# Expert weights in nine wide tiles with four neighbouring rows a partition, laid over the buffers of the part before them

## Chip, core and metric

The kernel runs on one core of a Trainium2 chip. Its time is the device time of one execution in microseconds (us); a kernel is told by the median of its runs, and its profile is of one execution. The engines are named PE (matmul), DVE, ACT and POOL (elementwise), and SP, whose queue issues nearly all DMA transfers; these are carried out by the core's 16 DMA engines. All arithmetic is in float32.

## What is computed

One layer over 256 latent tokens and 256 context tokens of width 1024. Cut to what matters here:

```
mod  = silu(c) @ w_ada + b_ada                       # w_ada 1024 x 6144
z    = modulate(rms_norm(x)) @ w_in                  # w_in 1024 x 2048, also for the context
conv = silu(layer_norm(dwconv31(z0 * sigmoid(z1))))
lru  = (scan forward + scan backward)(z2, start state from the context) * gelu(z3)
x    = x + g1 * (concat(conv, lru) @ w_out)          # w_out 1024 x 1024
h2   = modulate(rms_norm(x))
top group of 4, top 2 of its 8 experts, gates
y2[t] = sum over the 2 experts e of t: gate * (silu(h2 @ w1[e]) * (h2 @ w3[e])) @ w2[e]
out  = rms_norm(x + g2 * y2)
```

There are 32 experts. Each of w1[e], w3[e] and w2[e] is 1024 x 1024, that is 4 MB, so that an expert has 12 MB and all of them 384 of the 445 MB that the core moves.

## The kernel before

**The prelude** is everything up to the router's choice: modulation, w_in, convolution, scans, w_out, router, and the gather of the tokens of the first four experts. Its order is written out by hand in the string `ORDER`, in which a letter is a step. The steps that matter here: `b` loads 1 MB of w_ada and multiplies it (line 504; the first modulation's loads are those of line 235), `s`, `t` and `i` are tap products of the convolution, `z` a projection for the gelu (line 310), `Q` and `R` the variance and the row scales of the layer norm (lines 588 and 161), `q` a square root on ACT, `n` a scan on DVE (lines 426 to 430), `L`, `I`, `J` load w_out and split it into a high and a low part (the split of line 298, for the low part on POOL), `O` the output projection (line 675), `B` brings the scales into the gather's layout (line 627), `G` and `U` gather (line 810). The instructions of each engine, and the transfers in SP's queue, run in that order; an instruction waits only for what it reads and for the buffer that it writes.

**The buffers.** All large tiles come from one pool `wp` of SLOTS = 19 tiles `slot` of 128 partitions by 2048 floats, 8 KB a partition or 1 MB, in turn. The prelude uses them for weights and for intermediate values; the experts go on in the same ring, so that a load of an expert waits for the last reader of the tile 19 allocations earlier.

**The experts** are passed in order. Experts 0 to 30 each make twelve loads of 1 MB (`up`, line 845: four for w1, four for w3, four for w2), all with

```
w = slot().rearrange("p (k n) -> p k n", k=2)
dma(w, w_d[e, k2 * 256:(k2 + 1) * 256, :].rearrange("(p k) n -> p k n", p=128))
```

Partition p so holds rows 2p and 2p + 1 of 256, which lie next to each other in memory: one run of 8 KB. The gather (`pair`, `gather_mm`) brings the tokens' columns into the same order. The matmuls of line 848 use four row pieces of a load. Tokens are gathered into `xg` for four experts at a time, and results are added to x by a matmul with a selection matrix (line 870). SP's queue has eight completion semaphores for its transfers, DMAHW0 to DMAHW7; a transfer waits until the one eight before it has landed, so at most eight are on their way.

At the end of expert 1 the largest count of tokens in an expert is reduced to one number, `fmi` (lines 1002 to 1008). At the start of what follows, `nc.values_load(fmi...)` (line 1010) reads it into a register on the engines, SP among them; it decides whether a rarely needed second part for crowded experts is run. Behind it in SP's queue stand the load of `fg` (line 1013) and the loads of expert 3 on.

**Expert 31** is cut finer, for a short tail: w1 and w3 in halves of the columns (`up_half`, line 1032, 16 loads of 512 KB in runs of 2 KB), w2 in four loads of 512 KB of whole rows (line 1080) and four of 512 KB in column pieces (`part`, line 1089, runs of 1 KB). Between them PE finishes a piece, and DVE, ACT and POOL the normalisation of its columns.

Of the kernel before, what the change touches and what calls it, by code (L numbers as in the profile page):

```python
# [7 lines left out]
F32 = mybir.dt.float32  # L8
# [7 lines left out]
D = 1024  # L16
# [5 lines left out]
SLOTS = 19  # L22
# [8 lines left out]
v0 v1 h0 h1 o0 l0 t*2 v3 o1 t*3 v2 u0 l3 t*2 l1 l2 u1 t*2 b t s t s t*2 b t s t*2 s t s*3 t s*2 t s t i t s t s*2 t i  # L31
t*2 c1 t*2 b t s*2 t*3 s*2 t s b s*3 t*2 c0 b s*2 u2 s c2 s p10 s i p00 b a10 t*2 i*3 a00 u3 t p11 t s t w i t*3 b p01
t p20 s c3 s t s t s p30 t*2 d10 s t s*2 i t*2 a20 s*2 a30 t b t d00 t p21 a01 t r1 b t*2 s q10 t d30 i t d20 i b s b
t*2 s L0 q30 s q20 t s t*3 q00 z0 t L4 t b z1 t i p31 t*2 n00 s t*2 n20 d01 M a11 a31 k1 I0 C2 L2 z2 n10 C1 a21 I2 C0
C3 d21 d11 b q21 q11 q01 d31 Q z3 b R n01 e0 N1 L6 N2 x X1 N0 b X2 N3 I4 X3 b n30 n11 X0 m0 J0 J2 O001 e3 O002 J4 O100
q31 O111 O102 O112 O000 O011 e1 O012 I6 O010 O003 g n21 n31 O110 e2 O113 J6 j m1 X5 O101 m3 m2 X4 X7 X6 r2 O103 O005
O007 O013 O006 O105 O004 O015 O106 k2 O016 O114 O104 O017 O014 O107 D00 O115 D01 y H00 Y0 D10 O117 O116 H01 H10 D11
K00 H11 K01 Z0 K10 K11 T0 P0 F0 G06 B G04 G02 G00 Y1 T1 G07 P1 Z1 G03 F1 G01 G05 G10 G11 G12 G16 G14 A1 U0 G17 G15 U1
U4 G13 U2 U3 U6 U5 A0 U7
# [7 lines left out]
LNSQ = "SGGG"  # L47
XC = ("SS", "SV")
WH, WL = "VSVS", "VVGV"
MH, ML = "VSSGGSSG", "GVGGGVVG"  # L50
# [12 lines left out]
NSP = _n  # L63
# [3 lines left out]
def hybrid_layer(ctx: ExitStack, tc: tile.TileContext, sp_d, x_d, c_d, bada_d, rb_d, fg_d, gw_d,  # L67
                 wada_d, win_d, wout_d, w1_d, w3_d, w2_d, out_d):
    nc = tc.nc
    V, S, G, P = nc.vector, nc.scalar, nc.gpsimd, nc.tensor  # L70
    dma = nc.sync.dma_start

    const = ctx.enter_context(tc.tile_pool(name="const", bufs=1))
    wp = ctx.enter_context(tc.tile_pool(name="wp", bufs=SLOTS))
# [5 lines left out]
    def slot():  # L80
        return wp.tile([128, 2048], F32, name="slot")

    ctx.enter_context(tc.manual_schedule())
# [3 lines left out]
    sp = const.tile([128, NSP], F32, name="sp")  # L87
# [6 lines left out]
    bada = const.tile([48, 128], F32, name="bada")  # L94
# [9 lines left out]
    xn = const.tile([128, 2, D], F32, name="xn")  # L104
# [83 lines left out]
    silc = const.tile([128, 8, 32], F32, name="silc")  # L188
# [126 lines left out]
    pt = ada_turn(ada_rows(pa))  # L315
# [289 lines left out]
    wrs = const.tile([128, 8, 36], F32, name="wrs")  # L605
# [17 lines left out]
    def paired():  # L623
        pt = bank()
        for i in range(2):
            for h in range(2):
                P.matmul(pt[64 * h:64 * h + 64, i * 8:(i + 1) * 8], ident[:, i::2], gs[:, :, h::2],
                         start=i == 0, stop=i == 1, skip_group_check=True, tile_position=(0, 64 * h))
        S.copy(gsp.rearrange("p j (a i) -> p i j a", i=2), pt[:, 0:16].rearrange("p (i j a) -> p i j a", i=2, j=2))
# [149 lines left out]
    def pair(k):  # L779

        return slice(k // 2 * 256 + k % 2, k // 2 * 256 + 256, 2)

    def gather_mm(pg, i, k, oh, t):
        P.matmul(pg[:, i * 256:(i + 1) * 256], xn[:, t, pair(k)],  # L784
                 oh[:, t].rearrange("p e s -> p (e s)"), start=t + i == 0, stop=t == 1 and i == 1,
                 skip_group_check=True)
# [30 lines left out]
    def route(t):  # L817
# [7 lines left out]
                 g=g1_rows, B=paired, I=wo_hi, J=wo_lo, X=mixt_split, Z=first_split, y=second, x=router_row, j=router_rows, L=load_wo, O=oproj, W=warm,  # L825
# [12 lines left out]

    mo = ctx.enter_context(tc.tile_pool(name="mo", bufs=2, reuse_waits="tile"))

    def up(w_d, e, xs):
        ps = bank()
        for k2 in range(4):
            w = slot().rearrange("p (k n) -> p k n", k=2)
            dma(w, w_d[e, k2 * 256:(k2 + 1) * 256, :].rearrange("(p k) n -> p k n", p=128))
            for i in range(2):
                for h in range(2):
                    P.matmul(ps[64 * h:64 * h + 64, :], xs(k2 * 2 + i), w[:, i, h * 512:(h + 1) * 512],  # L848
                             start=k2 + i == 0, stop=k2 * 2 + i == 7, tile_position=(0, 64 * h))
        return ps  # L850
# [31 lines left out]
    def rest(base):  # L882
        pcs = mo.tile([128, 2, E], F32, name="pcs", bufs=1)
        V.tensor_scalar(pcs, posm, -float(base), None, OP.add)
        with tc.For_i(0, E) as ev:
# [3 lines left out]
            aux = slot()  # L889
# [6 lines left out]
            xg = slot()[:, 0:1024].rearrange("p (k s) -> p k s", k=8)  # L896
# [6 lines left out]
            def prod(w_d, xs):  # L903
                ps = [bank(), bank()]
                for k2 in range(4):
                    w = slot().rearrange("p (k n) -> p k n", k=2)
                    dma(w, w_d[bass.ds(ev, 1), k2 * 256:(k2 + 1) * 256, :].rearrange("o (k p) n -> p (o k) n", p=128))
                    for i in range(2):
                        for h in range(2):
                            P.matmul(ps[h], xs[:, k2 * 2 + i], w[:, i, h * 512:(h + 1) * 512],  # L910
                                     start=k2 + i == 0, stop=k2 * 2 + i == 7)
                return ps

            gg = slot()[:, 0:1024]
            gt = slot()[:, 0:1024].rearrange("p (k s) -> p k s", k=8)
            yy = slot()[:, 0:1024]
# [24 lines left out]
    for e in range(E - 1):  # L941
# [33 lines left out]
        for j in range(4):  # L975
            P.transpose(pt[:, j * 128:(j + 1) * 128], gg[:, pair(j)], ident)  # L976
# [34 lines left out]
        if e == 2:  # L1011
            fgr = slot()[0:1, 0:D]
            dma(fgr, fg_d)
            for j in range(2):
                pr = bank()
                P.matmul(pr, ones[0:1, :], fgr[:, j * 512:(j + 1) * 512], start=True, stop=True)
                S.copy(fgbc[:, j * 512:(j + 1) * 512], pr)
# [5 lines left out]
    ots = slot().rearrange("p (t d) -> p t d", t=2)  # L1023
    sqr = slot()
    e = E - 1

    def up_half(w_d, b):
        ps = bank()
        for k4 in range(2):
            w = slot().rearrange("p (k n) -> p k n", k=4)  # L1030
            for j in range(2):
                dma(w[:, 2 * j:2 * j + 2], w_d[e, k4 * 512 + j * 256:k4 * 512 + j * 256 + 256, b * 512:(b + 1) * 512]
                    .rearrange("(p i) n -> p i n", p=128))
            for i in range(4):
                for h in range(2):
                    P.matmul(ps[64 * h:64 * h + 64, 0:256], xg[:, k4 * 4 + i, 3 * CAP:],
                             w[:, i, h * 256:(h + 1) * 256], start=k4 + i == 0, stop=k4 * 4 + i == 7,
                             tile_position=(0, 64 * h))
        return ps
# [37 lines left out]
    for f2 in range(2):  # L1077
        w = slot().rearrange("p (k n) -> p k n", k=2)
        for f in range(2):
            dma(w[:, f], w2_d[e, (f2 * 2 + f) * 128:(f2 * 2 + f + 1) * 128, :])  # L1080
            for i, (c0, n) in enumerate(CUTS):
                down(i, f2 * 2 + f, w[:, f, c0:c0 + n])
        if f2 == 0:
            turn_half(1)

    def part(i):
        c0, n = CUTS[i]
        w = slot()[:, 0:4 * n].rearrange("p (k n) -> p k n", n=n)
# [54 lines left out]
    def final():  # L1143
        for t in range(2):
            m = mo.tile([128, 2], F32, name="m")
            ot = slot()[:, 0:D]
# [52 lines left out]
```

## Time and profile before

| | |
|---|---|
| median of 3 runs | 1142.86 us (1141.5 to 1144.75) |
| the profiled execution | 1141.62 us |
| its span in the profile | 1139.8 us |
| moved in it | 445.25 MB, mean 391 GB/s |
| PE busy | 89% of the span |

The span is what the engines' records cover; 1.8 us of the execution lie around it. The page of the profile gives busy times over the whole span, and the views by stretch, by wait and by chain of the same execution give them place by place. GB/s are of 16 engines together.

### The profile page before, as it was taken

Reading aid. Unit: us, or ns where it says so; the run is one execution under the profiler, and the core shown is the slowest. Engines: PE = TensorE matmul, PEld = TensorE weight load, DVE = VectorE, ACT = ScalarE, POOL = GpSimd, SP = SyncE. Lnnn points to the kernel's source line nnn. Section 1 sums busy time; section 2 is a strip of 40 time slices with the busy share of each in tenths; the row PEclk is TensorE's granted clock in tenths of the full one; section 3 lists DMA queues with packets and bytes.
Section 4 is the critical chain, followed back from the end, with each engine's and each line's share of the span. In section 5 each row is a group of like instructions: output and inputs, shape, how many; then the busy total and the mean of one; then the engine's idle time right before and its main releaser. Section 6 shows DMA issues by size and latency. Waiting matters only on the chain.

```text
span 1139.8 us, 12269 instructions
## 1 busy us (share of the span) xinstructions
PE 1015.8 (89%) x4923; PEld 420.9 (37%) x4923; DVE 309.8 (27%) x628; ACT 172.7 (15%) x325; POOL 103.0 (9%) x108
## 2 busy tenths in 40 slices
PE   7899998999999888888898988988888888888796
PEld 6764646333443323223232323232323232322234
DVE  4889966111122121111211121112011211111113
ACT  3467934100000000000000000000000000000002
POOL 2487432000000000000000000000000000000001
PEclk9899998999999999999999999999999999999999
DMA  9958696989999999999999999999999999999995
GB/s 347 310 215 340 239 405 273 392 351 421 419 420 420 420 420 418 421 419 420 420 419 420 420 420 420 419 418 419 420 420 420 419 419 420 419 420 421 419 393 189
DMA packets 76930, 445.25 MB, mean 391 GB/s; under 512 B 7187, under 2 KB 17475, under 8 KB 27204
## 3 DMA queue, kind: packets, MB, share of 16 engines
q1 hardware_dynamic: 76658, 443.85, 95.5%
q8 instruction: 41, 0.67, 0.2%
q10 hardware_dynamic: 210, 0.55, 0.1%
q14 instruction: 21, 0.17, 0.0%
HBM read 443.32 MB, written 1.05 MB: 390 GB/s over the span
## 4 chain that ended last, share of the span: by engine, by line
DMA 68%; PE 22%; DVE 6%; issue 1%; ACT 1%; POOL 1%; SPq 0%; DVEq 0%; ACTq 0%; POOLq 0%
DMA slot<-in_w_dram 68%; PE bank L848 11%; PE bank L675 2%; PE bank L372 2%; DVE bank L464 1%; PE bank L870 1%; PE bank L784 1%; PE bank L326 1%; PE bank L506 1%; DVE slot L288 1%; PE bank L810 1%; DVE lw L213 0%; PE bank L310 0%; DVE g1s L268 0%; POOL slot L298 0%
## 5 line engine op out<-in xcount | busy, mean ns | idle before, releaser
L848 PE MATMUL bank<-slot 128*64 128x512 f32 x1984 | 469.4, 601 | 82.7 <-DMA slot<-in_w_dram 82.5
L848 PEld LDWEIGHTS bank<-slot 128*64 128x64 f32 x1984 | 129.4, 136 | 406.3 <-DMA slot<-in_w_dram 195.2
L848 PE MATMUL bank<-slot,gt 128*64 128x512 f32 x992 | 220.4, 596 | 3.6 <-DMA slot<-in_w_dram 2.6
L959 DVE TENSOR_TENSOR sl<-sl,bank 128x512 f32<-128x512 f32 x31 | 21.3, 687 | 491.6 <-issue 468.0
L848 PEld LDWEIGHTS bank<-slot,gt 128*64 128x64 f32 x992 | 68.1, 137 | 144.8 <-issue 133.0
L995 DVE TENSOR_TENSOR yy<-bank,g2bc 64x512 f32<-64x512 f32 x62 | 42.7, 689 | 194.6 <-PE bank L848 194.1
L1116 POOL TENSOR_TENSOR slot<-x,fgbc 128x256 f32<-128x256 f32 x6 | 4.3, 731 | 935.2 <-DVE x L1113 935.2
L952 ACT ACTIVATE sl<-bank 128x512 f32<-128x512 f32 x31 | 18.5, 597 | 456.6 <-PE bank L848 456.6
L870 PE MATMUL bank<-yy,st 128*128 128x512 f32 x120 | 58.0, 606 | 0.0
L784 PE MATMUL bank<-oh,xn 128*128 128x256 f32 x224 | 54.6, 387 | 0.0
L784 PEld LDWEIGHTS bank<-oh,xn 128*128 128x128 f32 x224 | 41.9, 197 | 14.7 <-issue 11.4
L979 ACT COPY gt<-bank 128x256 f32<-128x256 f32 x31 | 11.6, 373 | 221.6 <-DVE gt L978 221.6
L875 DVE TENSOR_TENSOR x<-x,bank 128x512 f32<-128x512 f32 x60 | 39.8, 683 | 7.1 <-PE bank L870 7.1
L790 ACT ACTIVATE slot<-bank,gsp 128x256 f32<-128x256 f32 x32 | 17.8, 564 | 150.6 <-PE bank L784 148.9
L298 POOL TENSOR_TENSOR slot<-slot 128x2048 fp32r<-128x2048 f32 x7 | 32.4, 4631 | 31.0 <-ACT slot L293 23.5
L326 PE MATMUL bank<-slot 128*128 128x256 f32 x192 | 28.7, 309 | 6.1 <-ACT slot L287 4.8
L870 PEld LDWEIGHTS bank<-yy,st 128*128 128x128 f32 x120 | 20.6, 191 | 26.5 <-issue 23.2
L326 PEld LDWEIGHTS bank<-slot 128*128 128x128 f32 x192 | 26.5, 212 | 8.1 <-ACT slot L287 5.8
L793 DVE TENSOR_SCALAR slot<-bank,gsp 128x256 f32<-128x256 f32 x32 | 17.3, 543 | 41.0 <-ACT slot L790 41.0
L976 PEld LDWEIGHTS bank<-ident,sl 128*128 128x128 f32 x124 | 19.4, 201 | 11.1 <-issue 7.1
L372 PE MATMUL bank<-slot 128*128 128x512 f32 x96 | 22.8, 393 | 0.2 <-POOL slot L298 0.2
L482 POOL TENSOR_TENSOR xn<-xn,fgbc 128x256 f32<-128x256 f32 x30 | 22.4, 747 | 3.6 <-DVE fgbc L479 1.0
(249 smaller groups left out, 687.6 us busy)
## 6 DMA issues: line engine op xcount, KB each, us to landing
slot<-in_w_dram SPq DMA_DIRECT2D x372, 1024.0 KB, 19.9
slot<-in_wada_dram SPq DMA_DIRECT2D x16, 1024.0 KB, 6.9
slot<-in_w_dram SPq DMA_DIRECT2D x24, 512.0 KB, 10.8
slot<-in_wada_dram SPq DMA_DIRECT2D x16, 512.0 KB, 10.8
slot<-in_win_dram SPq DMA_DIRECT2D x8, 1024.0 KB, 9.7
slot<-in_wout_dram SPq DMA_DIRECT2D x4, 1024.0 KB, 10.4
x<-in_x_dram SPq DMA_DIRECT2D x2, 512.0 KB, 4.2
slot<-in_ctx_dram SPq DMA_DIRECT2D x2, 512.0 KB, 6.5
```

The lines of the kernel that those rows point to most:

```text
L298: en.tensor_tensor(lo, w, f(hi), OP.subtract)
L326: P.matmul(pvg[ct][:, i * T:(i + 1) * T], wz[k // 2][wi][:, k % 2, c:c + 128], x[k // 4][:, k % 4, 0:T], start=k + i + n == 0, stop=k == 7 ...
L372: P.matmul(pu, w, x[k // 4][:, k % 4], start=k + n == 0, stop=k == 7 and n == 2)
L482: G.tensor_tensor(acc, acc, p, OP.add)
L675: P.matmul(p, m[:, q], w[:, c:c + 512], start=first and n == 0, stop=len(done) == 8 and n == len(passes) - 1)
L784: P.matmul(pg[:, i * 256:(i + 1) * 256], xn[:, t, pair(k)], oh[:, t].rearrange("p e s -> p (e s)"), start=t + i == 0, stop=t == 1 and i == ...
L848: P.matmul(ps[64 * h:64 * h + 64, :], xs(k2 * 2 + i), w[:, i, h * 512:(h + 1) * 512], start=k2 + i == 0, stop=k2 * 2 + i == 7, tile_positi ...
L870: P.matmul(pz, st[:, t * 128:(t + 1) * 128], yy[:, h * 512:(h + 1) * 512], start=True, stop=True)
L875: V.tensor_tensor(x1[:, t, q], x1[:, t, q], pz, OP.add)
L959: V.tensor_tensor(gg, sl, pb, OP.mult)
L976: P.transpose(pt[:, j * 128:(j + 1) * 128], gg[:, pair(j)], ident)
L995: V.tensor_tensor(yy[o:o + 64, h * 512:(h + 1) * 512], py[64 * h:64 * h + 64, :], g2bc[64 * h:64 * h + 64, h * 512:(h + 1) * 512], OP.mult)
```

## The change

Four things are changed.

1. **Wide tiles.** The prelude's pool `wp` has 17 slots, and it is closed, with the prelude's other pools `tmp` and `big`, after the last step. A new pool `wx` of nine tiles `wide0` to `wide8`, 128 by 4096 floats (16 KB a partition, 2 MB), is laid over the same memory, and is used in the turn that `WORDER` gives. `up` makes two loads of 2 MB in place of four of 1 MB; a partition holds four neighbouring rows, one run of 16 KB. The layout of the gathered tokens follows (`pair` becomes `quad`, `paired` becomes `quads` with 16 small matmuls in place of 4).
2. **Other tiles move** to make the room: `xg` gets a pool of its own, `sp`, `bada`, `silc` and `wrs` go to `big`, `fg` is loaded straight into `fgbc`, and the tail's tiles come from `xg`'s pool or from `mo`.
3. **The last expert** makes its half loads in pieces of wide tiles: `up_half` one load of 1 MB in place of two of 512 KB, with the same runs of 2 KB.
4. **The order** of the prelude's 333 steps is another, and some copies and products change engines (`i` products of DVE 11 to 7, `s` products of ACT 42 to 46; `LNSQ`, `XC` and entries of `WH`, `WL`, `MH`, `ML`).

```diff
-SLOTS = 19
+SLOTS = 17
+WIDE = 9
+WORDER = (0, 7, 5, 2, 1, 6, 4, 3, 8)
...
-C3 d21 d11 b q21 q11 q01 d31 Q z3 b R n01 e0 N1 L6 N2 x X1 N0 b X2 N3 I4 X3 b n30 n11 X0 m0 J0 J2 O001 e3 O002 J4 O100
+C3 d21 q11 b q21 q01 d31 z3 Q n01 b R e0 N1 N2 X1 N0 I2 L6 x b X2 N3 X0 n30 J2 J0 O001 e3 q31 O112 I4 e2 X3 n11 I6
...
-LNSQ = "SGGG"
-XC = ("SS", "SV")
+LNSQ = "SGSG"
+XC = ("VS", "SV")
...
-    wp = ctx.enter_context(tc.tile_pool(name="wp", bufs=SLOTS))
+    xgp = ctx.enter_context(tc.tile_pool(name="xgp", bufs=2))
+    pro = ExitStack()
+    wp = pro.enter_context(tc.tile_pool(name="wp", bufs=SLOTS))
+    tmp = pro.enter_context(tc.tile_pool(name="tmp", bufs=2))
+    big = pro.enter_context(tc.tile_pool(name="big", bufs=1))
...
-    def paired():
+    def quads():
         pt = bank()
-        for i in range(2):
-            for h in range(2):
-                P.matmul(pt[64 * h:64 * h + 64, i * 8:(i + 1) * 8], ident[:, i::2], gs[:, :, h::2],
-                         start=i == 0, stop=i == 1, skip_group_check=True, tile_position=(0, 64 * h))
+        for i in range(4):
+            for h in range(4):
+                P.matmul(pt[32 * h:32 * h + 32, i * 4:(i + 1) * 4], ident[:, i::4], gs[:, :, h::4],
+                         start=i == 0, stop=i == 3, skip_group_check=True, tile_position=(0, 32 * h))
...
-    def pair(k):
-        return slice(k // 2 * 256 + k % 2, k // 2 * 256 + 256, 2)
+    def quad(k):
+        return slice(k // 4 * 512 + k % 4, k // 4 * 512 + 512, 4)
...
     pro.close()
+    wx = ctx.enter_context(tc.tile_pool(name="wx", bufs=1, reuse_waits="tile"))
     mo = ctx.enter_context(tc.tile_pool(name="mo", bufs=2, reuse_waits="tile"))
+    turn = [0]
+    def wide():
+        n = WORDER[turn[0] % WIDE]
+        turn[0] += 1
+        return wx.tile([128, 4096], F32, name=f"wide{n}")
...
     def up(w_d, e, xs):
         ps = bank()
-        for k2 in range(4):
-            w = slot().rearrange("p (k n) -> p k n", k=2)
-            dma(w, w_d[e, k2 * 256:(k2 + 1) * 256, :].rearrange("(p k) n -> p k n", p=128))
-            for i in range(2):
+        for k4 in range(2):
+            w = wide().rearrange("p (k n) -> p k n", k=4)
+            dma(w, w_d[e, k4 * 512:(k4 + 1) * 512, :].rearrange("(p k) n -> p k n", p=128))
+            for i in range(4):
                 for h in range(2):
...
-            fgr = slot()[0:1, 0:D]
-            dma(fgr, fg_d)
+            dma(fgbc[0:1, :], fg_d)
...
     def up_half(w_d, b):
         ps = bank()
         for k4 in range(2):
-            w = slot().rearrange("p (k n) -> p k n", k=4)
-            for j in range(2):
-                dma(w[:, 2 * j:2 * j + 2], w_d[e, k4 * 512 + j * 256:k4 * 512 + j * 256 + 256, b * 512:(b + 1) * 512]
-                    .rearrange("(p i) n -> p i n", p=128))
+            w = piece(2048).rearrange("p (k n) -> p k n", k=4)
+            dma(w, w_d[e, k4 * 512:(k4 + 1) * 512, b * 512:(b + 1) * 512].rearrange("(p i) n -> p i n", p=128))
```

Two places of the order matter below. The first is SP's queue at the hand-over from the prelude to the experts (`in_wada` is w_ada, `in_wout` w_out, `in_w` the experts' weights; in brackets the semaphores that a transfer waits for: PE, DVE, Activation and Pool for those engines). Before:

```order
L649 DMA slot<-in_wout_dram 128x2x1024 [waits DMAHW1_49,PE_49]
L504 DMA slot<-in_wada_dram 128x2048 [waits DMAHW2_49,PE_49]
L504 DMA slot<-in_wada_dram 128x2048 [waits DMAHW3_49,PE_49]
L845 DMA slot<-in_w_dram 128x2048 [waits DMAHW4_49,DVE_49,Activation_49]
L845 DMA slot<-in_w_dram 128x2048 [waits DMAHW5_49,PE_49]
L845 DMA slot<-in_w_dram 128x2048 [waits DMAHW6_49]
L845 DMA slot<-in_w_dram 128x2048 [waits DMAHW7_49,DMAHW0_49,PE_49]
L845 DMA slot<-in_w_dram 128x2048 [waits DMAHW2_49,PE_49]
L845 DMA slot<-in_w_dram 128x2048 [waits DMAHW1_49,DVE_49,Pool_49]
```

And after:

```order
L654 DMA slot<-in_wout_dram 128x2x1024 [waits DMAHW4_49,PE_49]
L509 DMA slot<-in_wada_dram 128x2048 [waits DMAHW5_49,DMAHW2_49,PE_49]
L509 DMA slot<-in_wada_dram 128x2048 [waits DMAHW3_49,PE_49]
L874 DMA wide_1747<-in_w_dram 128x4096 [waits PE_49,Pool_49]
L874 DMA wide_1757<-in_w_dram 128x4096 [waits Activation_49]
L874 DMA wide_1781<-in_w_dram 128x4096 [waits DMAHW2_49,DVE_49,DMAHW6_49,PE_49,Activation_49]
L874 DMA wide_1791<-in_w_dram 128x4096 [waits DMAHW7_49,PE_49]
L874 DMA wide_1811<-in_w_dram 128x4096 [waits DMAHW0_49,PE_49]
L874 DMA wide_1821<-in_w_dram 128x4096 [waits DMAHW1_49,DVE_49,Activation_49]
L874 DMA wide_1839<-in_w_dram 128x4096
L874 DMA wide_1849<-in_w_dram 128x4096 [waits DMAHW3_49,PE_49]
L874 DMA wide_1862<-in_w_dram 128x4096 [waits DMAHW4_49,PE_49,Pool_49]
```

The first expert load waited for DVE and ACT before, and waits now for PE and POOL, behind one more transfer of w_ada; the ninth wide load waits for PE and POOL, and each one after it for PE alone.

The second place is PE around the layer norm's variance: line 310 (315 in the changed kernel) is the projection z, 588 (593) the variance, 506 (511) a w_ada step, 161 (166) the row scales, 572 (577) the mean. Before:

```order
L572 MATMUL bank<-xn,ones 128x256 x4
L520 MATMUL bank<-ident,t_1141 128x128 x4
L310 MATMUL bank<-slot 128x256 x8
L506 MATMUL bank<-slot,silc 32x512 x4
L588 MATMUL bank<-ones,g2bc 128x1 x8
L310 MATMUL bank<-slot 128x256 x8
L506 MATMUL bank<-slot,silc 32x512 x4
L161 MATMUL bank<-ident,r 128x128 x2
L633 MATMUL bank<-rb,ones 1x36
```

And after:

```order
L577 MATMUL bank<-xn,ones 128x256 x4
L511 MATMUL bank<-slot,silc 32x512 x4
L525 MATMUL bank<-ident,t_1177 128x128 x4
L315 MATMUL bank<-slot 128x256 x8
L511 MATMUL bank<-slot,silc 32x512 x4
L315 MATMUL bank<-slot 128x256 x8
L593 MATMUL bank<-ones,g2bc 128x1 x8
L511 MATMUL bank<-slot,silc 32x512 x4
L166 MATMUL bank<-ident,r 128x128 x2
L638 MATMUL bank<-rb,ones 1x36
```

Both halves of the last projection now stand ahead of the variance, and a w_ada step stands between it and the row scales.

## Rows read from the trace of the kernel before

**Rows 1.** The page: busy time, chain, packets, issues (count, size, us to landing).

```profile
PE 1015.8 (89%) x4923; PEld 420.9 (37%) x4923; DVE 309.8 (27%) x628; ACT 172.7 (15%) x325; POOL 103.0 (9%) x108
...
DMA packets 76930, 445.25 MB, mean 391 GB/s; under 512 B 7187, under 2 KB 17475, under 8 KB 27204
...
DMA slot<-in_w_dram 68%; PE bank L848 11%; PE bank L675 2%; PE bank L372 2%; DVE bank L464 1%; PE bank L870 1%; PE bank L784 1%; PE bank L326 1%; PE bank L506 1%; DVE slot L288 1%; PE bank L810 1%; DVE lw L213 0%; PE bank L310 0%; DVE g1s L268 0%; POOL slot L298 0%
...
slot<-in_w_dram SPq DMA_DIRECT2D x372, 1024.0 KB, 19.9
slot<-in_wada_dram SPq DMA_DIRECT2D x16, 1024.0 KB, 6.9
...
x<-in_x_dram SPq DMA_DIRECT2D x2, 512.0 KB, 4.2
```

**Rows 2.** Busy time by stretch: length, each engine, granted clock, DMA share, GB/s.

```profile
140.00:190.00 50.00, 45.99 (x211) 27.96 (x211) 31.76 (x61) 21.52 (x41) 17.46 (x20) 0.91 0.93 378
190.00:200.00 10.00, 10.00 (x51) 5.87 (x52) 6.05 (x25) 4.04 (x11) 1.57 (x2) 0.85 0.33 113
200.00:247.00 47.00, 43.80 (x205) 16.56 (x203) 8.36 (x19) 5.58 (x10) 0.00 (x0) 1.00 0.93 378
250.00:1083.00 833.00, 746.91 (x3190) 256.65 (x3186) 138.08 (x262) 47.40 (x100) 0.00 (x0) 1.00 1.01 420
1083.00:1124.00 41.00, 36.32 (x276) 18.05 (x276) 7.06 (x14) 1.67 (x5) 0.00 (x0) 1.00 1.00 373
20.50:24.50 4.00, 3.52 (x73) 2.87 (x69) 3.15 (x19) 2.30 (x4) 0.40 (x1) 1.00 1.09 347
1096.00:1112.00 16.00, 13.78 (x108) 6.82 (x106) 2.09 (x4) 0.86 (x3) 0.00 (x0) 1.00 1.05 389
```

**Rows 3.** Chain that ended last: start us, us, what (two places).

```profile
340.98 19.89 DMA slot<-in_w_dram
...
360.93 19.89 DMA slot<-in_w_dram
...
1101.82 10.81 DMA slot<-in_w_dram
...
1112.69 10.69 DMA slot<-in_w_dram
```

**Rows 4.** Timeline of SP's queue: start us, us, engine line, transfer, count.

```profile
30.19 5.22 SPq L235 DMA_DIRECT2D slot<-in_wada_dram  x4
...
139.78 91.19 SPq L845 DMA_DIRECT2D slot<-in_w_dram  x36
246.97 0.31 SPq L1013 DMA_DIRECT2D slot<-in_fg_dram  x1
247.37 12.96 SPq L845 DMA_DIRECT2D slot<-in_w_dram  x12
```

**Rows 5.** What SP's queue waited for, 130 to 260: total us, times, longest.

```profile
SPq L1010 <- DVE so L856: 15.5, 1, 15.5
...
SPq L845 <- DVE slot L416: 11.6, 1, 11.6
```

**Rows 6.** Timelines of POOL and DVE: start us, us, engine line, op, shape, count.

```profile
35.04 4.60 POOL L298 TENSOR_TENSOR slot<-slot 128x2048 fp32r<-128x2048 f32 x1 [6.42 <-ACT slot L293]
...
147.09 4.84 POOL L298 TENSOR_TENSOR slot<-slot 128x2048 fp32r<-128x2048 f32 x1 [4.13 <-DVE slot L295]
...
147.59 4.88 DVE L426 TENSOR_TENSOR_SCAN slot<-slot 128x256 f32<-128x256 f32 x1
```

**Rows 7.** Timeline of PE, in the same columns.

```profile
48.22 1.96 PE L239 MATMUL bank<-slot,silc 128*32 128x128 f32 x64
...
189.39 4.52 PE L810 MATMUL bank<-oh,t 128*128 128x256 f32 x22
193.84 7.09 PE L848 MATMUL bank<-slot 128*64 128x512 f32 x32
```

More of the change, by code (lines that the diff above doesn't have):

```diff
@@ L185, in hybrid_layer @@
     first_norm(0, x1)
-    silc = const.tile([128, 8, 32], F32, name="silc")
+    silc = big.tile([128, 8, 32], F32, name="silc")
     G.memset(silc, 0.0)
@@ L836, in hybrid_layer, with pieces, piece @@
     pro.close()
+    wx = ctx.enter_context(tc.tile_pool(name="wx", bufs=1, reuse_waits="tile"))
     mo = ctx.enter_context(tc.tile_pool(name="mo", bufs=2, reuse_waits="tile"))
+    turn = [0]
[3 more added lines that the diff above has]
+        return wx.tile([128, 4096], F32, name=f"wide{n}")
+    for n in range(WIDE):
+        wx.tile([128, 4096], F32, name=f"wide{n}")
+    def pieces():
+        left = [None, 0]
+        def piece(n):
+            if left[1] < n:
+                left[:] = [wide(), 4096]
+            a = 4096 - left[1]
+            left[1] -= n
+            return left[0][:, a:a + n]
+        return piece
     def up(w_d, e, xs):
         ps = bank()
[L843 to L846 removed]
+        for k4 in range(2):
+            w = wide().rearrange("p (k n) -> p k n", k=4)
+            dma(w, w_d[e, k4 * 512:(k4 + 1) * 512, :].rearrange("(p k) n -> p k n", p=128))
+            for i in range(4):
                 for h in range(2):
[L848 to L849 removed]
+                    P.matmul(ps[64 * h:64 * h + 64, :], xs(k4 * 4 + i), w[:, i, h * 512:(h + 1) * 512],
+                             start=k4 + i == 0, stop=k4 * 4 + i == 7, tile_position=(0, 64 * h))
         return ps
@@ L888, in rest @@
             V.tensor_copy(pc[:, :, 1:2], gate[:, :, bass.ds(ev, 1)])
-            aux = slot()
+            aux = wide()
             oh = aux[:, 0:256].rearrange("p (t s) -> p t s", t=2)
@@ L895, in rest @@
                 V.tensor_scalar(so[:, t], oh[:, t], pc[:, t, 1:2], None, OP.mult)
-            xg = slot()[:, 0:1024].rearrange("p (k s) -> p k s", k=8)
+            xg, gg, gt = (aux[:, (i + 1) * 1024:(i + 2) * 1024] for i in range(3))
+            xg, gt = (v.rearrange("p (k s) -> p k s", k=8) for v in (xg, gt))
+            yy = wide()[:, 0:1024]
             for k in range(8):
@@ L904, in prod @@
                 ps = [bank(), bank()]
[L905 to L908, printed above, removed]
+                for k4 in range(2):
+                    w = wide().rearrange("p (k n) -> p k n", k=4)
+                    dma(w, w_d[bass.ds(ev, 1), k4 * 512:(k4 + 1) * 512, :].rearrange("o (k p) n -> p (o k) n", p=128))
+                    for i in range(4):
                         for h in range(2):
-                            P.matmul(ps[h], xs[:, k2 * 2 + i], w[:, i, h * 512:(h + 1) * 512],
-                                     start=k2 + i == 0, stop=k2 * 2 + i == 7)
-                return ps
-            gg = slot()[:, 0:1024]
-            gt = slot()[:, 0:1024].rearrange("p (k s) -> p k s", k=8)
-            yy = slot()[:, 0:1024]
+                            P.matmul(ps[h], xs[:, k4 * 4 + i], w[:, i, h * 512:(h + 1) * 512],
+                                     start=k4 + i == 0, stop=k4 * 4 + i == 7)
+                return ps
             pa = prod(w1_d, xg)
@@ L1022, in hybrid_layer @@
     ms = mo.tile([128, 2, n_cut + 1], F32, name="ms", bufs=1)
-    ots = slot().rearrange("p (t d) -> p t d", t=2)
-    sqr = slot()
+    ots = xgt().rearrange("p (t d) -> p t d", t=2)
+    sqr = mo.tile([128, 256], F32, name="sqr", bufs=1)
+    piece = pieces()
     e = E - 1
@@ L1145, in final @@
             m = mo.tile([128, 2], F32, name="m")
-            ot = slot()[:, 0:D]
+            ot = wide()[:, 0:D]
             S.activation(ot, x1[:, t], AF.Square, accum_out=m[:, 0:1])
```

51 lines of the change are left out of this document (25 added, 26 removed).

## The prediction

> **What bounds the kernel now.** I read the page first. TensorE is busy for 89% of the span, which looks like the bound; but the chain that ended last lies 68% in DMA into `slot` from the expert weights [rows 1]. An average over a prelude and a stream says little, so the next view is the busy time by stretch [rows 2]. From 250 to 1083 us the 16 DMA engines have a share of 1.01 and move 420 GB/s, while PE works 746.9 of 833 us. Twenty-eight experts of 12 MB pass there: 833/28 = 29.75 us of transfer for each against 26.7 us of PE. The stream is limited by the bytes and by what the engines spend on each of them; a shorter PE time would be worth nothing there. Before 250 us the engines have room: a share of 0.93, a hole of 0.33 between 190 and 200, again 0.93.
>
> Whether that hole costs time decides what a faster start would be worth. The SP queue sends the first expert load at 139.78 and 36 of them by 231; then it stops until 246.97 [rows 4], since it waits 15.5 us at line 1010 for DVE [rows 5]: `values_load` on SP reads `fmi`, which is computed at the end of expert 1. The 36 loads are experts 0 to 2. While SP waits, the last of them land and the engines run dry. At 247.37 the queue sends again, cold, and from there the engines are full to the end. So the time has two parts: **what ends expert 1 on PE**, and after it **336 MB plus the last expert**. How early the first 36 MB come is worth nothing as long as PE is not short of them and they have landed by about 247.
>
> **Part 1: 16-KB rows.** A load of 1 MB puts 128 rows of 8 KB on 16 engines, eight rows each. A load goes out when the one eight before it has landed, so the chain steps from one batch of eight to the next: the steps start 19.95 us apart [rows 3], which is 64 rows per engine, 311.7 ns a row. The last expert shows shorter rows: eight loads of 512 KB in 2-KB rows take 10.87 us [rows 3], which is 128 rows per engine at 84.9 ns. A line through both gives 37.8 ns for each KB and 9.3 ns for each row. Its check is the 1-KB loads of the prelude: 347 GB/s over 16 engines [rows 2] is 47.2 ns a row, and the line says 47.1. A 16-KB row would then take 614 ns in place of 623.4 for two of 8 KB. After the restart there are 372 - 36 = 336 loads of 1 MB [rows 1], now 168 of 2 MB, eight long rows per engine in each: 1344 rows that save 9.3 ns, **12.5 us**. From the rates alone (420 and 389 GB/s [rows 2]) the row's constant is 8.3 ns and the saving 11.2 us. The bounds are 0 (a long row is as dear as two) and 16 (constants of about 12 ns, if the curve bends). I take 12.5, since three row lengths lie on one line.
>
> [...]
>
> The last expert's loads keep rows of 2, 4 and 1 KB, though some are joined; from 1083 us on I count nothing. PE has the same matmuls in the loop. It now waits for 2 MB and not for 1 MB before it starts on a tile; since it needs 26.7 us where the transfers need 29.3, that delay is inside slack, and the last wide tile lands 40 us of other loads before the end.
>
> **Part 2: fewer buffers in flight.** Nine tiles of 16 KB hold 18 MB, as against 19 slots. At the restart expert 2 fills six tiles, so three loads can go out at once, and each tile that PE frees (some 26.7/6 = 4.5 us apart) admits another, against 4.9 us for a transfer. Two or three are always on their way. Cost: 0, and a few us if fewer than eight loads do not fill the engines.
>
> **Part 3: the first expert loads.** A wide tile lies over two prelude slots and more, so it waits for the last reader of all of them. Before, the first load waited for `slot` of line 416 [rows 5] and left at 139.78 [rows 4]. Now it waits for the second half of z3 and for the low split of w_out on POOL, which took 147.09 + 4.84 = 151.9 [rows 6]: I put it at 153. Eighteen wide loads at 4.91 us end near 153 + 88 + 2 = 243, before 247. That margin of 3 or 4 us is all: each us after 156 delays the restart's equal, but hides here. The ninth tile waits for the last gather matmul, that is for 193.8 [rows 7]; the queue behind it waits too, and the eight tiles ahead of it need 39 us, to 194. PE needs its seventh tile only 26 us after its start. Cost: 0, up to 4 us.
>
> **Part 4: the reordered prelude.** PE starts the experts at 193.84 after the last 4.52 us of gather matmuls [rows 7]; the end of expert 1, and with it the restart, moves one for one with that start. Two slots less make early loads wait. The four w_ada loads sent at 30.19 [rows 4] now wait for the first low split on POOL, which ends at 35.04 + 4.60 = 39.6 [rows 6]. The last would land near 48, and PE wanted it at 48.22 [rows 7]. Other loads of the prelude go 1 to 11 us later, all still ahead of their use by this reckoning. On the gain side, z3 stands ahead of Q on PE, so that PE need not idle for the variance; four products move from DVE to ACT; and POOL's split of 4.84 us, beside which a scan on DVE took 4.88 [rows 6], now stands ahead of the product behind which it stood, so that it may fall beside other work. On the cost side, `quads` has 16 tiny matmuls in place of 4, under 1 us. **Sum: -0.5 us**, from -2 to +4.
>
> **The sum.** 1141.6 us (the profiled execution) - 12.5 - 0.5 = 1128.6. The median of the runs is 1.2 us above that execution, so the forecast for the median is **1129.8 us**; from 1124 to 1134 with the bounds of the parts.
>
> **The rivals.**
> *No gain from longer rows.* The page counts 49,726 packets of 8 KB and more (76,930 less 27,204), about the 388 loads with 8-KB rows times 128 = 49,664 [rows 1]: one packet for a row. If 8 KB is the longest that the engines take at once, a 16-KB row becomes two packets and nothing is saved. The trace has no longer row to exclude it. Then 1142.9 - 0.5 = 1142.4. Against it stands only that nothing in 1, 2 and 8 KB shows a limit. Chance 0.12.
>
> *Half a gain.* [...] Chance 0.16.
>
> *Slower: the prelude starves with 17 slots.* PE takes the w_ada tiles in order, and the w_out and w_in loads stand behind them in one SP queue. A load that is sent cold takes 4.2 us for 512 KB [rows 1] and 6.9 for 1 MB [rows 1] to land. If the margins of part 4 (0.2 us in the tightest place) are gone, PE waits at each such place, the slots then come free later, and the next load is later again. Every us of that moves the start of the experts, the end of expert 1 and the restart. It decides from 12.5 - 0.5 + 3.4 = 15.4 us: three or four such waits of 4 to 7 us. Four times 5.5 is 22 us, less 12.5: 1152. For it: the prelude's DMA is not idle, and some 40 loads pass through 17 slots; against it: the moves in the order send the loads ahead of use nearly everywhere. Chance 0.10.
>
> **Chances.** The forecast's case (1124 to 1134) has 0.62. A measurement of this kernel can tell about 0.3%, 3.4 us, from no change, so no change means 1139.5 to 1146.3. Faster takes the forecast and nearly all of half a gain: 0.77. No change takes no gain and the edge of the others: 0.13. Slower: 0.10. The range that leaves out two cases in ten goes from 1123, a little beyond the lower bound, to 1141, which takes in half a gain and the near side of no gain, and leaves out the slow case.
>
> **What the profile would show.** Right: DMA at about 425 or 426 GB/s in the stream in place of 420, a wide load every 4.91 us; `fmi` still waited for by SP, the fg load near 246 to 247, and then the same distance to the end less 12.5. No gain: the same 4.99 us for 2 MB. Starved: idle time of PE before lines 239 and 506 of the old numbering that ends on a DMA, and an expert start well after 194. The forecast is wrong in its base if SP is no longer stopped by `fmi`, or if DMA's share in the stream falls below 1 with PE as the releaser.

## The result, and the profile after

The changed kernel takes **1125.13 us** (median of 4 runs, 1121.9 to 1126.55) against 1142.73 of the kernel before in the same runs; the ratio is 0.984, 95% interval 0.9814 to 0.9867. That is 17.6 us less; 13 were forecast, and the range held. The profiled execution took 1124.29 us, its span is 1122.5.

The page of the changed kernel, its lines on busy time, packets and the wide loads, against [rows 1]:

```profile
PE 1001.9 (89%) x4947; PEld 447.2 (40%) x4947; DVE 308.7 (27%) x625; ACT 173.7 (15%) x329; POOL 104.1 (9%) x107
...
DMA packets 50015, 445.21 MB, mean 397 GB/s; under 512 B 4083, under 2 KB 14371, under 8 KB 24100
...
wide<-in_w_dram SPq DMA_DIRECT2D x186, 2048.0 KB, 38.7
```

The packets fell from 76,930 to 50,015, and those of 8 KB and more from 49,726 to 25,915 (50,015 less 24,100), so a row of 16 KB is one packet. That alone sets aside the rival by which 8 KB is the longest that an engine takes at once.

Busy time by stretch, as in [rows 2] (length, each engine, granted clock, DMA share, GB/s):

```profile
190.00:200.00 10.00, 10.00 (x55) 8.71 (x50) 4.84 (x20) 6.54 (x13) 2.69 (x2) 0.69 0.83 333
248.00:253.00 5.00, 3.18 (x17) 1.08 (x17) 2.91 (x9) 0.00 (x0) 0.00 (x0) 1.00 0.14 60
250.00:1067.00 817.00, 735.62 (x3203) 280.81 (x3203) 139.36 (x268) 47.56 (x100) 0.00 (x0) 1.00 1.00 429
1067.00:1107.00 40.00, 36.81 (x290) 20.27 (x291) 7.43 (x16) 1.67 (x5) 0.00 (x0) 1.00 0.98 381
600.00:1000.00 400.00, 356.26 (x1550) 137.66 (x1546) 69.58 (x132) 22.47 (x47) 0.00 (x0) 1.00 1.01 431
```

The stream runs at 429 GB/s and not 420, and in the middle, 600 to 1000 us, at 431. The last expert, for which I had counted nothing, is faster too: 381 against 373. The hole between 190 and 200 is nearly gone (0.83 against 0.33), and another, at 248 to 253, has stayed (0.14).

SP's queue, its timeline and what it waited for, against [rows 4] and [rows 5]:

```profile
155.40 78.19 SPq L874 DMA_DIRECT2D wide<-in_w_dram  x18
251.77 0.31 SPq L1040 DMA_DIRECT2D fgbc<-in_fg_dram  x1
```

```profile
SPq L874 <- PE bank L815: 19.1, 1, 19.1
SPq L1038 <- DVE so L885: 17.7, 1, 17.7
...
SPq L874 <- POOL slot L303: 13.7, 1, 13.7
```

The first wide load waits 13.7 us for POOL's low split, the ninth 19.1 us for the last gather matmul, and the queue stops 17.7 us for `fmi`, all as the order had it. The end of the prelude on PE, against [rows 7]:

```profile
192.82 5.42 PE L815 MATMUL bank<-oh,t 128*128 128x256 f32 x22
198.18 7.09 PE L877 MATMUL bank<-wide,xg 128*64 128x512 f32 x32
```

The experts start 4.3 us **later** than in the profiled execution of the kernel before, and the restart after `fmi` comes 4.8 us later (251.77 against 246.97). So the gain lies wholly behind the restart. From the load of fg to the end of the span the kernel before takes 1139.8 - 246.97 = 892.8 us, the changed one 1122.5 - 251.77 = 870.7: **22.1 us less**, where 12.5 were forecast. This distance, free of the prelude, is used below as "the rest".

### The profile page after: what moved, and what is told of

Its sections match the earlier page's. It is cut to its first block, busy times and chain, and to the rows that moved or that the text cites. A ratio compares the mean times of both kernels' runs of the same rounds, so it can differ in the third digit from the quotient of the medians.

```text
span 1122.5 us, 11836 instructions
## 1 busy us (share of the span) xinstructions
PE 1001.9 (89%) x4947; PEld 447.2 (40%) x4947; DVE 308.7 (27%) x625; ACT 173.7 (15%) x329; POOL 104.1 (9%) x107
## 2 busy tenths in 40 slices
DMA packets 50015, 445.21 MB, mean 397 GB/s; under 512 B 4083, under 2 KB 14371, under 8 KB 24100
## 4 chain that ended last, share of the span: by engine, by line
DMA 57%; PE 33%; DVE 5%; POOL 1%; issue 1%; ACT 1%; SPq 1%; DVEq 0%; POOLq 0%; ACTq 0%
DMA wide<-in_w_dram 57%; PE bank L877 18%; PE bank L789 3%; PE bank L680 2%; PE bank L899 2%; PE bank L377 2%; PE bank L331 1%; PE bank L511 1%; DVE bank L469 1%; PE bank L815 1%; PE bank L315 1%; DVE slot L293 1%; PE bank L1004 1%; POOL slot L303 1%; SPq L1059 1%
## 5 line engine op out<-in xcount | busy, mean ns | idle before, releaser
L877 PE MATMUL bank<-wide,xg 128*64 128x512 f32 x1984 | 448.4, 596 | 78.6 <-DMA wide<-in_w_dram 78.5
L877 PEld LDWEIGHTS bank<-wide,xg 128*64 128x64 f32 x1984 | 141.4, 137 | 370.1 <-issue 256.7
L877 PE MATMUL bank<-wide,gt 128*64 128x512 f32 x992 | 219.9, 595 | 2.9 <-DMA wide<-in_w_dram 2.3
L877 PEld LDWEIGHTS bank<-wide,gt 128*64 128x64 f32 x992 | 68.6, 137 | 141.8 <-issue 137.4
L1142 POOL TENSOR_TENSOR xg<-x,fgbc 128x256 f32<-128x256 f32 x6 | 4.2, 728 | 914.1 <-DMA wide<-in_w_dram 912.8
L789 PE MATMUL bank<-oh,xn 128*128 128x256 f32 x224 | 61.1, 416 | 0.0
L789 PEld LDWEIGHTS bank<-oh,xn 128*128 128x128 f32 x224 | 54.4, 327 | 11.4 <-issue 11.4
L795 ACT ACTIVATE xg<-bank,gsp 128x256 f32<-128x256 f32 x32 | 17.9, 564 | 153.7 <-PE bank L789 149.2
L798 DVE TENSOR_SCALAR xg<-bank,gsp 128x256 f32<-128x256 f32 x32 | 17.2, 543 | 47.3 <-ACT xg L795 47.2
```

The lines of the kernel that those rows point to most:

```text
L789: P.matmul(pg[:, i * 256:(i + 1) * 256], xn[:, t, quad(k)], oh[:, t].rearrange("p e s -> p (e s)"), start=t + i == 0, stop=t == 1 and i == ...
L877: P.matmul(ps[64 * h:64 * h + 64, :], xs(k4 * 4 + i), w[:, i, h * 512:(h + 1) * 512], start=k4 + i == 0, stop=k4 * 4 + i == 7, tile_positi ...
```

## The experiments

All variants compute the whole layer. What puzzled was a detail of the two traces: rows whose loads were not touched had become shorter as well, a 1-KB row of the prelude 46.2 ns on the mean and not 50.5 (loads in the first 39 us), a 2-KB row of the last expert 84.2 and not 88.3. (The time of a row is that of its transfer record in the trace.)

**1. The kernel before, again, beside the variants.**

> The kernel before, again, for its trace beside those of the variants. The changed kernel's trace has shorter transfers even where the same loads are made as before (a 1-KB row of the prelude 46 ns and not 50, a 4-KB row 159 and not 164). Theory A (the rate is the row length's): here too the short rows of the prelude show the times of the changed kernel's trace, 46 and 159 ns, the difference being one of the two executions, and the stream keeps 420 GB/s; about 1142 us. Theory B (the difference of the two traces is one of execution or chip, not of the kernel): 46 and 159 ns and a stream of about 425 GB/s or more, so that part of what the traces show as gain is none. Theory C (the kernel before slows all its transfers, whatever their shape): 50 and 164 ns again.

1140.98 us (one run). The stream, in the view by stretch:

```profile
600.00:1000.00 400.00, 354.96 (x1506) 122.62 (x1508) 67.22 (x126) 22.38 (x47) 0.00 (x0) 1.00 1.01 420
```

1-KB rows take 50.5 ns again, 8-KB rows 315.1; the rest is 1139.2 - 245.54 = 893.7. So the kernel before has longer times for its short rows in this execution too: theory C. Neither the one execution nor the length of a row alone explains the difference.

**2. Rows of 8 KB in loads of 2 MB.**

```diff
-            dma(w, w_d[e, k4 * 512:(k4 + 1) * 512, :].rearrange("(p k) n -> p k n", p=128))
+            dma(w.rearrange("p (c k n) -> p c (k n)", c=2), w_d[e, k4 * 512:(k4 + 1) * 512, :]
+                .rearrange("(c p k) n -> p c (k n)", c=2, k=2))
```

with `pair`, `paired` and the split half loads of the kernel before.

> The changed kernel with two rows of 8 KB a partition in each load of 2 MB (two blocks of 256 rows), the gather laid out for them as before, and the last expert's half loads of 512 KB as before. Number of loads as in the changed kernel, length of rows as before. Theory A (a row costs some 9 to 14 ns beside its bytes): the stream falls back to 420 GB/s, 168 x 8 x 9 to 14 ns x 1 = 12 to 20 us come back: 1138 to 1146 us. Rival (a load costs, not a row): the stream stays at 430 GB/s, 1124 to 1128 us, with up to 2 us from the tail's split loads.

1127.83 us (1124.5 to 1129.97), ratio to before 0.9853 (0.9821 to 0.9884). Theory A's forecast is missed. The time lies inside the rival's, at its upper end; experiment 3 decides on the rival. The stream:

```profile
600.00:1000.00 400.00, 352.25 (x1540) 130.63 (x1534) 69.59 (x132) 22.36 (x47) 0.00 (x0) 1.00 1.01 427
```

With rows as long as before it moves 427 GB/s, and an 8-KB row takes 309.4 ns, not 315. In these tiles the length of the row is worth the step from 427 to 431 GB/s and no more.

**3. Rows of 8 KB in loads of 1 MB.**

```diff
+            src = w_d[e, k4 * 512:(k4 + 1) * 512, :].rearrange("(p k) n -> p k n", p=128)
+            for j in range(2):
+                dma(w[:, 2 * j:2 * j + 2], src[:, 2 * j:2 * j + 2])
```

> The changed kernel with each wide tile filled by two loads of 1 MB, each with the 8-KB half of every partition's 16 KB. Rows and loads as before, tiles, order and gather as changed. Theory A: as the variant with 8-KB rows in 2-MB loads, 1138 to 1146 us. Rival (a load costs): 1138 to 1146 as well. If neither holds and the gain lies in the tiles or in the order, it stays at 1125. Against the variant with 2-MB loads it tells what twice the loads cost at one row length: 0 by theory A, 15 to 20 us by the rival.

1130.53 us (1129.06 to 1131.7), ratio 0.9885 (0.986 to 0.9909). The stream:

```profile
600.00:1000.00 400.00, 362.32 (x1538) 130.57 (x1534) 69.58 (x132) 22.43 (x47) 0.00 (x0) 1.00 1.01 427
```

Again 427, and the rest is 877.3 against 877.8 in the experiment before: **twice as many loads cost nothing** in the stream, and the rival of experiment 2 is out. (The medians are 2.7 us apart; the profiled restart came 1.2 us later here, with the gather in fours, and the rest of that difference was not followed up.) Rows and loads are those of the kernel before, and still it is some 13 us faster than that kernel's 1145.06 in the same runs. What is left is the tiles or the order; the next experiment tries where the tiles lie.

**4. Rows of 16 KB in loads of 1 MB**, each for 64 partitions.

```diff
+            src = w_d[e, k4 * 512:(k4 + 1) * 512, :].rearrange("(p k) n -> p k n", p=128)
+            for j in range(2):
+                dma(w[64 * j:64 * j + 64], src[64 * j:64 * j + 64])
```

> The changed kernel with each wide tile filled by two loads of 1 MB, each with 64 partitions in full rows of 16 KB. Length of rows as changed, loads as before. Theory A: 430 GB/s and 1123 to 1128 us. Rival (a load costs): 420 GB/s and 1138 to 1146 us. A third way: 64 partitions are worse spread than 128, and it falls below 420 GB/s, above 1146 us.

1771.1 us (1687.98 to 1848.95; the profiled execution 1790.42). The stream:

```profile
600.00:1000.00 400.00, 254.48 (x794) 90.47 (x792) 34.91 (x68) 12.34 (x26) 0.00 (x0) 0.79 1.01 219
```

The third way, and far beyond it: the engines are as busy (1.01) and move half. A row takes 1204 ns; why was not tried. As a test of the length of a row it is void; the other experiments had to settle that.

**5. Thirty-two bytes.** In the compiled programs the 19 slots of the kernel before begin at byte 52448 of a partition, 32 more than a multiple of 64 and 224 more than one of 256, since the constants ahead of them have odd sizes. In the changed kernel, where `sp`, `bada`, `silc` and `wrs` have left the constants and `xg` stands ahead, slots and wide tiles begin at 66048, a multiple of 512. So, in the kernel before alone:

```diff
+    pad = const.tile([128, 8], F32, name="pad")
     half = const.tile([128, 4], F32, name="half")
```

> The kernel before with one unused tile of 32 bytes a partition put among the constants, and nothing else: its 19 slots then begin at 52480 bytes of a partition (a multiple of 256) and not at 52448 (32 more than a multiple of 64). Theory D (a row that is written to an address off by 32 costs 5 to 6 ns more; this and not the wide tiles is most of the gain): 8-KB rows take 309 ns and not 315, 2688 rows per engine save 15 us, the tail and the prelude another 1 to 3: 1124 to 1128 us. Rival (the pools, the order or the wide tiles make the transfers shorter): 315 ns and 1142 to 1145 us.

1127.46 us (1124.42 to 1130.17) against 1141.53, ratio 0.9862 (0.9833 to 0.9891). The stream, and the load of fg:

```profile
600.00:1000.00 400.00, 361.01 (x1540) 124.35 (x1536) 69.61 (x132) 22.36 (x47) 0.00 (x0) 1.00 1.01 427
```

```profile
250.53 0.31 SPq L1014 DMA_DIRECT2D slot<-in_fg_dram  x1
```

An unused tile of 32 bytes gives **14 of the 17.6 us**. 8-KB rows take 309.4 ns; the rest is 1128.4 - 250.53 = 877.9, that is 15 to 16 us less than before, as 2688 rows x 5.7 ns say. Theory D holds, and the rival (pools, order or wide tiles) is out, since none of them is in this kernel.

**6. The changed kernel off by 32 bytes** (the same line added).

> The changed kernel with the same unused 32 bytes: its wide tiles then begin 32 bytes off a multiple of 64. Theory D with a cost for each row: the 16-KB rows lose 5 to 6 ns each, 1344 rows per engine 7 to 8 us, with the short rows about 10: 1133 to 1136 us. Theory D with a cost for each byte (2% of the time of a row, as 309 to 315): 623 ns a row, 16 us: 1140 to 1142 us. Rival: 611 ns, 1125 us.

1131.37 us (1130.54 to 1132.67), ratio 0.9903 (0.9882 to 0.9924):

```profile
600.00:1000.00 400.00, 354.04 (x1536) 137.00 (x1538) 67.55 (x127) 22.47 (x47) 0.00 (x0) 1.00 1.01 427
```

A 16-KB row takes 616.4 ns and not 611.7: 4.7 more, about as an 8-KB row has 5.7 and a 1-KB row 4.3 more. The cost is a **row's**, not a byte's; with half the rows a bad place costs half. 1344 x 4.7 = 6.3 us, and the median is 6.2 above the changed kernel's; the 1133 to 1136 us expected were too many. The rest became 9.2 us longer (879.9 against 870.7); short rows of the last expert pay too, and what remains is not accounted for.

**7. The changed kernel off by 64 bytes** (16 floats in place of 8).

> The changed kernel with 64 unused bytes: tiles at a multiple of 64, but 64 off a multiple of 128, 256 and 512. If 64 bytes are the step that counts, as fast as the changed kernel, 1122 to 1127 us and 611 ns; if 128, 256 or 512 are, as slow as with 32 bytes.

1130.54 us (1127.52 to 1131.57), ratio 0.9901 (0.9879 to 0.9923). 1-KB rows take 50.7 ns (in the first 39 us), 16-KB rows 615.5; a multiple of 64 is not enough. (The profiled execution, 1127.52, is the fastest: its experts started at 193.8, of which below.)

**8. Slots at a multiple of 128.**

```diff
+    pad = const.tile([128, 8], F32, name="pad")
...
-    wrs = const.tile([128, 8, 36], F32, name="wrs")
+    wrs = big.tile([128, 8, 36], F32, name="wrs")
```

> The kernel before with its slots at 51328 bytes of a partition: a multiple of 128 that is not one of 256 (the tile wrs moves from the constants to the prelude's big tiles, and the unused 32 bytes stay). If a multiple of 128 is enough: 8-KB rows of 309 ns, 1-KB rows of 46, and 1124 to 1130 us, as with slots at a multiple of 256. If 256 is wanted: 315 and 50 ns, and 1139 to 1144 us.

1139.24 us (1135.73 to 1142.27, 10 runs), ratio 0.9968 (0.9949 to 0.9987):

```profile
600.00:1000.00 400.00, 356.83 (x1516) 123.30 (x1516) 67.23 (x126) 22.37 (x47) 0.00 (x0) 1.00 1.01 421
```

8-KB rows take 313.9 ns, 1-KB rows 50.4. A multiple of 128 is nearly as slow as the old place, 224 bytes beyond a multiple of 256; a multiple of 256 that is not one of 512 (52480, experiment 5) is fast, 309.4 ns. The step that counts is **256 bytes**. That the extra grows with the distance from the boundary the rows do not show: 32, 64, 128 and 224 bytes beyond a multiple of 256 all cost 4 to 6 ns (32 and 64 measured with 16-KB rows, 128 and 224 with 8-KB rows).

**9. The order alone**: the kernel before with the 32 bytes, and with `ORDER`, `LNSQ`, `XC`, `WH`, `WL`, `MH`, `ML` of the changed one.

> The kernel before with the unused 32 bytes, and with the order of the changed kernel and its choice of engines; 19 slots, 1-MB loads and the gather for two rows stay. It shows what the order does to PE between the row scales of the layer norm, the router's first matmul behind the top-k, and the first expert. From row scales to that matmul the kernel before took 40.56 us in three traces, the changed one 42.57; from there to the first expert 9.7 to 9.8 and 10.9. If the order makes both longer: 42.5 and 10.9. If the 17 slots make the first and the gather for four rows the second: 40.6 and 9.8. If the order makes the first and the gather the second: 42.5 and 9.8. Time about 1127 us either way, with 2 or 3 us of spread.

1129.33 us (one run). From the row scales to the router's first matmul behind the top-k it takes 186.76 - 144.18 = 42.6 us, from there to the first expert 196.34 - 186.76 = 9.6: the order makes the first longer, the gather for four rows the second. Experiment 2, with the changed order and the gather in pairs, agrees: 42.55 and 9.8 us. Weight loads of the gather matmuls in the stream, first with rows in fours (the changed kernel), then in pairs (experiment 2), as the view by line has them:

```profile
L789 PEld LDWEIGHTS bank<-oh,xn 128*128 128x128 f32 x224 | 54.4, 327 | 11.4 <-issue 11.4
```

```profile
L789 PEld LDWEIGHTS bank<-oh,xn 128*128 128x128 f32 x224 | 41.8, 197 | 14.7 <-issue 11.4
```

A weight load that takes every fourth column needs 327 ns on the mean, every second 197. In the stream that is hidden (a rest of 877.3 in fours and 877.8 in pairs). At the end of the prelude it is not: the last 22 gather matmuls take 5.42 us in the changed kernel and 4.64 in experiment 2.

**10. `fmi` read later**, in the changed kernel and in the kernel before with the 32 bytes:

```diff
-        if e == 2:
+        if e == 10:
             nmax = nc.values_load(fmi[0:1, 0:1], min_val=0, max_val=T)
```

> The changed kernel with the reading of fmi into the registers at expert 10 instead of expert 2; nothing else moves. Theory (the stream stops because SP waits 17.7 us for fmi; DMA's share falls to 0.33 and 0.02 between 248 and 252): the stream goes on without a hole and 4 to 5 us are won, 1119 to 1122 us. Rival (the tiles, not SP, end the wait, since a tile comes free only when PE is through with it): no change, 1124 to 1127 us.

> The kernel before with the unused 32 bytes and with fmi read at expert 10. If the stop at fmi costs the same 4 to 6 us here: 1121 to 1124 us, and what is left of the wide tiles against it is the 2 to 4 us by which the changed kernel with the late reading (1119.7) is ahead. If the full slots between 190 and 200 us hold the stream up anyway, less is won: 1125 to 1128.

**1119.66 us** (1118.85 to 1120.85), ratio 0.9806 (0.9785 to 0.9828), and 1121.84 us (1120.5 to 1124.4), ratio 0.9825 (0.9792 to 0.9857). The hole of the changed kernel, 248 to 253 us, is filled, as the view by stretch of the late variant shows against the 0.14 above:

```profile
248.00:253.00 5.00, 4.08 (x19) 1.43 (x21) 2.08 (x8) 0.00 (x0) 0.00 (x0) 1.00 1.00 429
```

By the medians both win about 5.5 us, though of runs made at different times. From the start of the experts to the end of the span, free of the prelude, the profiled executions went from 924.3 to 920.1 us in the changed kernel and from 931.0 to 925.6 in the other, 4.2 and 5.4 less. The stop at `fmi` was real in both, and the changed kernel with the late reading is the fastest of all kernels here.

The rest (from the load of fg to the end of the span), with the mean time of a row in 300 to 1000 us by the trace's transfer records:

| kernel | tiles begin at, beyond a multiple of 256 | row | ns a row | rest, us |
|---|---|---|---|---|
| before (two traces) | 224 | 8 KB | 315.1 | 892.8, 893.7 |
| 8: slots at 128 | 128 | 8 KB | 313.9 | 889.8 |
| 5: before, 32 bytes | 0 | 8 KB | 309.4 | 877.9 |
| 9: the order, 32 bytes | 0 | 8 KB | 309.4 | 878.1 |
| 2: 2-MB loads | 0 | 8 KB | 309.4 | 877.8 |
| 3: 1-MB loads | 0 | 8 KB | 309.4 | 877.3 |
| 6: changed, 32 bytes | 32 | 16 KB | 616.4 | 879.9 |
| 7: changed, 64 bytes | 64 | 16 KB | 615.5 | 878.3 |
| changed | 0 | 16 KB | 611.7 | 870.7 |

Records of one engine overlap a little (a DMA share of 1.01), so twice 8 KB less 16 KB in this table, 13.8 ns at a bad place and 7.1 at a good one, overstates what a long row saves. By the rates of the stream (420 and 427 GB/s, 427 and 431) it is about 10 ns and 6, which 1344 rows turn into the differences of the rest.

## Why the prediction was right, and where it was not

The median, 1125.13 us, lies 4.7 below the forecast and inside its range, 1123 to 1141; that it does is in part luck, as two terms were wrong by 9 and 5 us in opposite directions. Of what the prediction named as signs of being right, only the stop of SP at `fmi` came: the stream ran at 429 GB/s and not at 425 or 426, the load of fg went at 251.77 and not near 246 to 247, and the distance from it to the end shrank by 22.1 us and not by 12.5.

**What bounds the kernel** held: the stream is limited by the transfers (a DMA share of 1.00, with PE busy for 735.6 of 817 us), SP stops 17.7 us at `fmi`, only what lies behind the restart counts, and a slower prelude is paid about one for one (experts 4.3 us later, restart 4.8). The late reading shows the same from the other side.

**Part 1, longer rows: right in size, for tiles at a bad address.** I had 12.5 us from a cost of 9.3 ns beside the bytes of a row. At the old kind of address, the step from 8-KB to 16-KB rows is 892.8 or 893.7 less 879.9, so 13 to 14 us. By the rates above, a long row saved about 10 ns there against the 9.3 forecast. But the 9.3 ns were two things in one: what a row costs anywhere, and what it costs because it begins beside a multiple of 256 bytes. The straight line through 2, 8 and 1 KB could not part them, since all its rows were written beside such a multiple. At a good address longer rows are worth 877.8 less 870.7, 7 us. Half a gain, which the chances (0.16) and the upper end of the range count in, is a term that no run shows; what the runs showed in its place are these 7 us at a good address and 13 to 14 at the old kind.

**The term that was missing** is the place of the tiles, which the change moved in passing, when it took `sp`, `bada`, `silc` and `wrs` out of the constants and put `xg` ahead of the slots: the prediction counted it at nothing. Beside the longer rows it is worth 878.3 or 879.9 (experiments 7 and 6) less 870.7, 8 to 9 us; by itself, with short rows, 15 to 16. It fell on all rows, and so on the last expert, where I had counted nothing.

**Part 2**, nine tiles at no cost: right. The share in the stream is 1.00, and the rest with nine wide tiles (877.3, 877.8) is that of 19 slots (877.9).

**Part 3**: I put the first wide load at 153, it went at 155.4 (behind two transfers of w_ada, as before, and not one more), and its cost was nothing: the engines run dry near 249, before the restart at 251.8, which itself came later than I had reckoned.

**Part 4 failed: -0.5 us, with bounds of -2 and +4, became +4.3** in the profiled execution. No place starved: ahead of the experts PE waits 0.6 us for tiles of w_ada, 1.5 before. The 4.3 us are 1.1 up to the row scales (144.72 against 143.58), 2.0 from there to the router (42.57 against 40.56) and 1.2 from there to the first expert (10.89 against 9.70). The last is the gather in fours, which I had as "under 1 us" for the small matmuls alone, without the slower weight loads: its last 22 matmuls take 5.42 us in place of 4.52.

The middle one has two causes. From the row scales to the first output projection PE takes 3.8 us in the changed kernel and 2.3 in experiment 7, which has the same order:

```profile
144.72 0.91 PE L166 MATMUL bank<-ident,r 128*128 128x128 f32 x4 [0.41 <-POOL r L160]
148.52 4.56 PE L680 MATMUL bank<-slot,xn 128*128 128x512 f32 x10
```

```profile
141.88 0.71 PE L167 MATMUL bank<-ident,r 128*128 128x128 f32 x4 [0.41 <-POOL r L161]
144.14 4.56 PE L681 MATMUL bank<-slot,xn 128*128 128x512 f32 x10
```

The granted clock between 140 and 160 us is 0.91 in the first and 1.00 in the second: in the first it is 0.55 from 144.72 to 148.52 us and 1.00 again between 150 and 160. The 3.8 us against 2.3 are 1.5 us. The other 0.5 remains where the clock did not fall (41.06 us in experiment 7) and goes to the order, since experiment 9 has the same 42.6 with the clock at 0.91. In the kernel before the clock fell too (0.83 between 134 and 144 us), but ahead of the row scales, in the second half of the projection z behind the variance. That half takes 5.39 us, at a clock of 0.68, and 3.70 in experiment 8, whose granted clock between 140 and 160 us is 1.00:

```profile
137.27 5.39 PE L310 MATMUL bank<-slot 128*128 128x256 f32 x16
```

So with the old order the distance from row scales to router is 40.5 to 40.6 us in all five traces, and a fall shows in the start of the row scales instead. The fall comes behind the variance in three of five traces with the old order (that half of z takes 5.4 to 6.7 us in these, 3.7 in the others) and in five of six with the new order and wide tiles (3.6 to 3.8 us from the row scales to the first output projection, 2.3 in the other), too few to say that the order brings it about; why it comes in some executions and not in others stays open.

The start of the experts differs by as much from run to run: 191.5 to 197.4 us over five traces with the old order, 193.8 to 198.2 over six with the new order and wide tiles (without experiment 4). On the means, 193.7 and 196.4, the change loses 2.8 us, all of it behind the row scales, which begin at 143.4 on both means. PE's wait of 0.78 us at the variance is gone, as I had counted on with z3 ahead of Q, but at the row scales no gain is left of it, nor of the products moved to ACT.

The sum as it should have been: rows -13, place -9, expert start +4 to +5, together -17 to -18. The errors of two terms cancelled in part; the range held, the reasons only in part. The slower rival had the right place (the start of the experts moves the end about one for one), but another mechanism. Its sum of 15.4 us has a sign wrong: part 4 was a gain there too, so 12.5 + 0.5 + 3.4 = 16.4; nothing hangs on it.

## What to carry to other kernels

Print where the tiles of a load-bound kernel begin in a partition: a multiple of 256 bytes was worth 14 us of 1142 here, at the price of an unused tile of 32 bytes a partition. When a fit over a trace gives a cost per row, ask what all its rows have in common before giving it to their length; and when a change moves tiles, treat their new addresses as part of the change. A register that is needed at the end should not be read in the middle by the queue that issues the loads; here that cost about 5.5 us.

## What the runs showed of the hardware that was not expected

A row written to SBUF at an address 32, 64, 128 or 224 bytes beyond a multiple of 256 takes 4 to 6 ns more: 16-KB rows 616.4 (32 bytes) and 615.5 ns (64) against 611.7, 8-KB rows 313.9 (128) and 315.1 (224) against 309.4, 1-KB rows 50.4 to 50.7 against 46.2, 2-KB rows 88.3 (224) against 84.2. A load of 2 MB and two of 1 MB cost the same in a full stream (427 GB/s both). Loads for 64 partitions at a time, with 16-KB rows, move 219 GB/s between 600 and 1000 us with the engines fully busy (1.01), half of what 128 partitions get (431). And with one and the same order the end of the prelude lies up to 6 us apart from run to run (191.5 to 197.4 us), more than the 2.8 us that the new order and gather cost; one fall of the granted clock (0.55 for 3.8 us) went with 1.5 us of it.
